# Raw output-weight loads issued from GpSimd's queue, and a seventh key buffer, in a one-core Trainium2 decoder layer

## The chip, the cores and the metric

The kernel runs on one core of one Trainium2 chip. The metric is device time in microseconds (us). A core has five engines with an instruction stream each: TensorE (PE in the profile; PEld are its weight loads), VectorE (DVE), ScalarE (ACT), GpSimd (POOL) and SyncE (SP). Each stream is worked off in order. An instruction may carry a wait for another engine or for a load, and everything behind it in the same stream waits too. In this kernel SP does nothing but issue loads and stores.

## The reference

One layer of a decoder trunk, on x of 2048 rows and 1024 columns, in float32. Cut to what matters here:

```python
h = rmsnorm(x, pre_norm_g)
q, k, v, g_attn, x_lru, g_lru = split(h @ w_in)          # 1024 columns each
y_attn = rmsnorm(diff_attention(q, k, v, lam)) * silu(g_attn)   # 8 heads, causal, two score maps a head
y_lru  = rg_lru(conv4(x_lru), gates) * silu(g_lru)        # 8 blocks of 128 channels
y = concat([y_attn, y_lru]) @ w_out                       # (2048, 2048) x (2048, 1024)
out = x + rmsnorm(y, post_norm_g)
```

## The kernel before

Every matmul operand is split into a high and a low part, and three products are added. Work is divided into 128-row tiles and 512-column chunks.

The kernel's stages, in order of time in the profile: normalisation and projections of the first half of the rows (0 to 600 us), the first half's attention with the second half's projections filled in between (to about 1144), the second half's recurrent part (`lru_run`, to 1382), the second half's attention with the output projection filled in between (1387 to about 2140), and the rest of the output projection (to the end).

Three things matter for the change.

*Output weights.* `load_wo(r, nh, k)` loads a tile of 128 rows and 512 columns into `woraw` (two buffers, line 950), and POOL splits it into `woh` (line 70) and `wol` (line 71). Eight of them (k = 0 to 7, one buffer each) are a set. There are four sets, in the order of `wsets`: (1, 0), (1, 1), (0, 0), (0, 1). The first is loaded beside the recurrent part (the program's scheduler moves it up to about 1144 us, the end of the first attention). Each other set is loaded during the last group of matmuls of the set before it, tile by tile as the old tile falls free, and the next group (line 1048, 24 matmuls in `fill_out`) reads it. The 49 groups run as fill between the attention's own instructions.

*Keys.* `load_k(h, j)` loads the keys of head h, positions 512 j to 512 j + 511, into one of `kbufs` buffers of the tag `ks`; a head has four such tiles in a ring. Scores (line 642) read them; the first score unit of a head in the second half reads tiles 0, 1 and half of tile 2 (that last matmul has 256 columns).

*Other work of POOL.* It splits the weights of the input projection (`wlo`, line 200, while DVE makes `whi`), the output projection's inputs (`yh`, `yl`, lines 70 and 71, in four parts a tile), and scales the attention's output (`yt`, line 782).

The order within each engine is fixed when the program is built: a scheduler places the instructions by its own model of their times and the buffers' availability. On the chip each engine keeps to that order.

Of the kernel before, what the change touches and what calls it, by code (L numbers as in the profile page):

```python
# [18 lines left out]
P = 128  # L19
S = 2048  # L20
D = 1024
KC = D // P
H = 8
CH = 512
# [10 lines left out]
FB = 8.25  # L35
# [8 lines left out]
def hymba_kernel(  # L44
# [6 lines left out]
    nc = tc.nc  # L51
    x2, out2, w_in2, w_out2 = x[0], out[0], w_in[0], w_out[0]
# [16 lines left out]
    def split(hi, lo, src):  # L69
        nc.gpsimd.tensor_scalar(out=hi, in0=src, scalar1=1.0, scalar2=1.0, op0=ALU.mult, op1=ALU.mult)  # L70
        nc.gpsimd.tensor_tensor(out=lo, in0=src, in1=hi.bitcast(F32), op=ALU.subtract)  # L71
# [875 lines left out]

    def load_wo(r, nh, k):
        raw = f_p.tile([P, CH], F32, tag="woraw", name="woraw", bufs=2)
        nc.sync.dma_start(out=raw, in_=w_out2[r * D + k * P:r * D + (k + 1) * P, nh * CH:(nh + 1) * CH])  # L950
        hi = f_p.tile([P, CH], F32R, tag=f"woh{k}", name=f"woh{k}", bufs=1)
        lo = f_p.tile([P, CH], F32R, tag=f"wol{k}", name=f"wol{k}", bufs=1)
        split(hi, lo, raw)
        wo[r, nh, k] = (hi, lo)

    def load_y(r, i):
        raw = f_p.tile([P, 8, P], F32, tag="yraw", name="yraw", bufs=YR)
        nc.sync.dma_start(out=raw, in_=(ya_s, yl_s)[r][i // 4][:, :, (i % 4) * P:(i % 4 + 1) * P])
        yh = f_p.tile([P, 8, P], F32R, tag="yh", name="yh")
        yl = f_p.tile([P, 8, P], F32R, tag="yl", name="yl")  # L960
        return (yh, yl), [(yh[:, k:k + 2], yl[:, k:k + 2], raw[:, k:k + 2]) for k in range(0, 8, 2)]
# [3 lines left out]
    def finish(pool, i, yv, bufs, halves, eng):  # L965

        ss = pool.tile([P, 6], F32, tag="ss", name="ss", bufs=6)

        def squares(c):
            s = slice(c * CH, (c + 1) * CH)  # L970
            junk = pool.tile([P, CH], F32, tag="fo", name="junk", bufs=bufs)
            nc.scalar.activation(out=junk, in_=yv[:, s], func=AF.Square, accum_out=ss[:, (5, 0)[c]:(6, 1)[c]])
            eng.tensor_tensor(out=yv[:, s], in0=yv[:, s], in1=pgt[:, s], op=ALU.mult)

        def rest():
            xt = pool.tile([P, D], F32, tag="xt", name="xt", bufs=bufs)
            nc.sync.dma_start(out=xt, in_=x2[i * P:(i + 1) * P, :])
            squares(0)
            nc.vector.tensor_tensor(out=ss[:, 0:1], in0=ss[:, 0:1], in1=ss[:, 5:6], op=ALU.add)
            rsqrt1(ss, D)  # L980
            for c0 in range(0, D, D // halves):
                s = slice(c0, c0 + D // halves)
                nc.vector.scalar_tensor_tensor(  # L983
                    out=xt[:, s], in0=yv[:, s], scalar=ss[:, 3:4], in1=xt[:, s], op0=ALU.mult, op1=ALU.add,
                )
                nc.sync.dma_start(out=out2[i * P:(i + 1) * P, s], in_=xt[:, s])

        squares(1)
        return rest

    with tc.tile_pool(name="lruB", bufs=2) as lp, tc.tile_pool(name="ps_pB", bufs=4, space=PSUM) as ps_p, \
            tc.tile_pool(name="ps_gB", bufs=1, space=PSUM) as ps_g:
        load_gw, lru_run = lru_tools(lp, ps_p, ps_g, 1)
        load_gw(0)
        pos = len(lightB)
        end = None
        for n in range(NB):
            wB.split(pos)
            wB.split(pos + 1)
            end = lru_run(n, wB, pos, end)  # L1000
            if n >= 4:
                load_wo(1, 0, 2 * (n - 4))
                load_wo(1, 0, 2 * (n - 4) + 1)
            pos += 2
        p1.close()
        end()
# [4 lines left out]
    with ExitStack() as pb:  # L1011
        kvB_p = pb.enter_context(tc.tile_pool(name="kvB", bufs=2, side="right"))
        e_p = pb.enter_context(tc.tile_pool(name="expB", bufs=2, side="right"))
        a_p = pb.enter_context(tc.tile_pool(name="attB", bufs=2, side="right"))
        ps_s = pb.enter_context(tc.tile_pool(name="ps_sB", bufs=4 * CH // SP, space=PSUM))
        ps_w = pb.enter_context(tc.tile_pool(name="ps_wB", bufs=2, space=PSUM))
        ps_o = pb.enter_context(tc.tile_pool(name="ps_oB", bufs=1, space=PSUM))
        ps_f = pb.enter_context(tc.tile_pool(name="ps_fB", bufs=1, space=PSUM))
        groups = [(r, nh, i) for r, nh in wsets for i in range((8, 16)[r])] + [(0, 1, 8)]

        def fill_out():
            ysp, parts = load_y(*groups[0][::2])
            for p in parts:
                split(*p)
            nc.sync.dma_start(out=pgt, in_=post_norm_g[0].partition_broadcast(P))
            for g, (r, nh, i) in enumerate(groups):
                ps = ps_f.tile([P, CH], F32, tag="f", name="f")
                yh, yl = ysp
                nxt = groups[g + 1] if g + 1 < len(groups) else None
                if nxt:  # L1030
                    ysp, parts = load_y(*nxt[::2])
                part = None
                c0 = nh * CH
                if i >= 8 and r == 0:
                    yv = f_p.tile([P, D], F32, tag="yv", name="yv", bufs=1)
                    nc.sync.dma_start(out=yv, in_=part_s[1][i])
                    part = yv[:, CH:]
                    ys[i], yvs[i] = ysp, yv
                elif r == 0:
                    if nh:  # L1040
                        yv = f_p.tile([P, D], F32, tag="yv", name="yv", bufs=1)
                        nc.sync.dma_start(out=yv[:, 0:CH], in_=part_s[0][i][:, 0:CH])
                    part = f_p.tile([P, CH], F32, tag="part", name="part", bufs=1)
                    nc.sync.dma_start(out=part, in_=part_s[1][i][:, c0:c0 + CH])
                for k in range(8):
                    hi, lo = wo[r, nh, k]
                    for m, (a, b) in enumerate(((yh, hi), (yl, hi), (yh, lo))):
                        nc.tensor.matmul(  # L1048
                            out=ps, lhsT=a[:, k, :], rhs=b, start=(k == 0 and m == 0), stop=(k == 7 and m == 2),
                        )  # L1050
                        if (k, m) != (7, 2):
                            yield
                    if nxt and nxt[:2] != (r, nh):
                        load_wo(*nxt[:2], k)
                    if k % 2 and nxt:
                        split(*parts[k // 2])
                if r == 0 and nh == 1:
                    nc.vector.tensor_tensor(out=yv[:, CH:], in0=ps, in1=part, op=ALU.add)  # L1058
                    ends[i] = finish(f_p, i, yv, 1, 1, nc.gpsimd if i < FE else nc.vector)
                    if i < 8:  # L1060
                        ends.pop(i)()
                else:
                    st = f_p.tile([P, CH], F32, tag="fo", name="fo", bufs=1)
                    if part:
                        nc.vector.tensor_tensor(out=st, in0=ps, in1=part, op=ALU.add)
                        nc.sync.dma_start(out=part_s[0][i][:, 0:CH], in_=st)
                    else:
                        nc.scalar.activation(out=st, in_=ps, func=AF.Copy)
                        nc.sync.dma_start(out=part_s[1][i][:, c0:c0 + CH], in_=st)
                yield "group"  # L1070

        attention(
            range(4, 8), kvB_p, e_p, a_p, ps_s, ps_w, ps_o, 4 * CH // SP, fill_out(),
            lambda s: FB if s > 1 else 6, 6, 5, 1,
        )


# [2 lines left out]
    with ExitStack() as p3:  # L1080
# [39 lines left out]
        for i in range(9, 12):  # L1120
            for k in ((0, 1, 2), (3, 4, 5), (6, 7))[i - 9]:
                raw = y_p.tile([P, CH], F32, tag="woraw3", name="woraw3")
# [45 lines left out]
```

## Time and profile before

| | |
|---|---|
| median of 3 runs | 2308.39 us (2305.96 to 2310.14) |
| the profiled execution | 2304.31 us, span 2302.5 us |
| PE busy | 2182.0 us, 95% |
| DVE busy | 1481.0 us, 64% |
| ACT busy | 984.2 us, 43% |
| POOL busy | 805.6 us, 35% |
| mean granted clock of PE | 0.981 of full |

The span is the profiled execution's; its own time is 1.8 us longer. Busy shares are means over stages. PE is the engine that is nearly always busy, so the rows below are about the stretches in which it is not, or in which its clock is at the lower of its two levels (1.2 instead of 2.4 GHz; 0.50 in the rows means that level throughout).

### The profile page before, as it was taken

Reading aid. Unit: us, or ns where it says so; the run is one execution under the profiler, and the core shown is the slowest. Engines: PE = TensorE matmul, PEld = TensorE weight load, DVE = VectorE, ACT = ScalarE, POOL = GpSimd, SP = SyncE. Lnnn points to the kernel's source line nnn. Section 1 sums busy time; section 2 is a strip of 40 time slices with the busy share of each in tenths; the row PEclk is TensorE's granted clock in tenths of the full one; section 3 lists DMA queues with packets and bytes.
Section 4 is the critical chain, followed back from the end, with each engine's and each line's share of the span. In section 5 each row is a group of like instructions: output and inputs, shape, how many; then the busy total and the mean of one; then the engine's idle time right before and its main releaser. Section 6 shows DMA issues by size and latency. Waiting matters only on the chain. (4 is left out here: it accounts for less than half of the span.)

```text
span 2302.5 us, 31830 instructions
## 1 busy us (share of the span) xinstructions
PE 2182.0 (95%) x11281; PEld 1800.5 (78%) x11281; DVE 1481.0 (64%) x2976; ACT 984.2 (43%) x2227; POOL 805.6 (35%) x773
## 2 busy tenths in 40 slices
PE   7999999999899999999999997999999997999778
PEld 6888888888677878888878775888788886887666
DVE  6531145446576666666337776888878886888565
ACT  4311134435443444444126564665565654555211
POOL 1222034445311111111275553133534335245452
PEclk9999999999999999999999998999999998999889
DMA  6554322332568777874462117457466475655473
GB/s 206 152 149 151 111 84 85 105 107 67 151 155 172 169 178 175 183 165 115 121 183 69 62 34 178 105 145 166 117 156 165 111 147 133 170 138 146 110 260 128
DMA packets 358783, 317.93 MB, mean 138 GB/s; under 512 B 32545, under 2 KB 290658, under 8 KB 358626
## 3 DMA queue, kind: packets, MB, share of 16 engines
q1 hardware_dynamic: 358626, 315.91, 52.8%
q8 instruction: 89, 1.46, 0.3%
q14 instruction: 68, 0.56, 0.1%
HBM read 221.41 MB, written 94.44 MB: 137 GB/s over the span
## 5 line engine op out<-in xcount | busy, mean ns | idle before, releaser
L228 PE MATMUL ps<-hh,whi 128*128 128x512 f32 (+1 forms) x1456 | 569.3, 391 | 3.7 <-DVE hilo L245 3.0
L228 PE MATMUL ps<-hh,wlo 128*128 128x512 f32 (+1 forms) x1456 | 567.1, 390 | 0.0
L228 PE MATMUL ps<-hl,whi 128*128 128x512 f32 (+1 forms) x1456 | 565.0, 388 | 1.1 <-DVE hl L446 1.1
L683 ACT ACTIVATE p<-s,nm 128x512 f32<-128x512 f32 (+3 forms) x640 | 392.0, 623 | 330.4 <-DVE nm L667 221.3
L665 DVE TENSOR_REDUCE mx<-s 128x1 f32<-128x512 f32 (+3 forms) x576 | 341.4, 618 | 115.4 <-PE s L642 95.3
L642 PE MATMUL s<-ks,qs 128*128 128x512 f32 (+2 forms) x1280 | 368.8, 386 | 33.7 <-DMA ks<-k_s 18.7
L200 POOL TENSOR_TENSOR wlo<-wraw,whi 128x1024 fp32r<-128x1024 f32 x88 | 222.5, 2529 | 438.6 <-DVE whi L199 136.3
L228 PEld LDWEIGHTS ps<-hh,whi 128*128 128x128 f32 x1456 | 277.3, 190 | 55.0 <-DVE hilo L245 3.8
L228 PEld LDWEIGHTS ps<-hl,whi 128*128 128x128 f32 x1456 | 276.9, 190 | 52.5 <-DVE hl L446 1.4
L228 PEld LDWEIGHTS ps<-hh,wlo 128*128 128x128 f32 x1456 | 276.6, 190 | 51.2
L642 PEld LDWEIGHTS s<-ks,qs 128*128 128x128 f32 x1280 | 215.7, 191 | 86.8 <-ACT p L683 36.3
L719 ACT ACTIVATE wh<-pw 128x512 fp32r<-128x512 f32 (+1 forms) x288 | 160.1, 577 | 184.9 <-PE pw L715 181.5
L738 PE MATMUL o<-wh,vs 128*128 128x256 f32 (+1 forms) x1152 | 223.5, 284 | 0.8 <-ACT wh L719 0.8
L720 DVE TENSOR_TENSOR wl<-pw,wh 128x512 fp32r<-128x512 f32 (+1 forms) x288 | 185.7, 654 | 35.9 <-ACT wh L719 34.6
L738 PEld LDWEIGHTS o<-wh,vs 128*128 128x128 f32 x1152 | 193.6, 192 | 19.1 <-ACT wh L719 3.3
L70 POOL TENSOR_SCALAR yh<-yraw 128x256 fp32r<-128x256 f32 x196 | 89.9, 476 | 288.8 <-PE f L1048 265.8
L1048 PE MATMUL f<-woh,yh 128*128 128x512 f32 x392 | 163.3, 417 | 22.1 <-DVE yv L1058 16.1
L782 POOL TENSOR_TENSOR yt<-yt,rb 128x512 f32<-128x512 f32 x32 | 41.8, 1307 | 406.0 <-DMA rb<-r_s 224.0
L701 DVE SCALAR_TENSOR_TENSOR p<-p,rr,p 128x128 f32<-128x128 f32 (+15 forms) x128 | 180.2, 1407 | 2.8
L715 PE MATMUL pw<-ident,p 128*128 128x128 f32 x1088 | 169.2, 274 | 4.1 <-DVE wl L720 2.6
L738 PE MATMUL o<-wl,vs 128*128 128x256 f32 x576 | 164.4, 286 | 9.1 <-DVE wl L720 9.1
L1048 PE MATMUL f<-wol,yh 128*128 128x512 f32 x392 | 163.3, 416 | 0.9 <-POOL wol L71 0.9
(166 smaller groups left out, 3316.9 us busy)
## 6 DMA issues: line engine op xcount, KB each, us to landing
wraw<-in_w_in_dram SPq DMA_DIRECT2D x96, 512.0 KB, 5.0
qs<-q_s SPq DMA_DIRECT2D x128, 256.0 KB, 5.5
vs<-v_s SPq DMA_DIRECT2D x48, 512.0 KB, 6.2
ks<-k_s SPq DMA_DIRECT2D x96, 256.0 KB, 5.6
xt<-in_x_dram SPq DMA_DIRECT2D x32, 512.0 KB, 4.7
k_s<-hilo SPq DMA_DIRECT2D x64, 256.0 KB, 4.1
q_s<-hilo SPq DMA_DIRECT2D x64, 256.0 KB, 3.8
v_s<-hilo SPq DMA_DIRECT2D x32, 512.0 KB, 3.7
```

Source lines behind the costliest of these rows:

```text
L70: nc.gpsimd.tensor_scalar(out=hi, in0=src, scalar1=1.0, scalar2=1.0, op0=ALU.mult, op1=ALU.mult)
L200: nc.gpsimd.tensor_tensor(out=lo, in0=src, in1=hi.bitcast(F32), op=ALU.subtract)
L228: nc.tensor.matmul(out=ps[:, t0:t0 + n], lhsT=a[:, k, :], rhs=b[:, k, t0:t0 + n], start=(k == 0 and m == 0), stop=(k == KC - 1 and m == 2),)
L642: nc.tensor.matmul(out=ps[:, b0 - c0:b0 - c0 + nk], lhsT=qq[:, c, t * P:(t + 1) * P], rhs=kst[h, b0 // CH][:, c, 0:nk], start=(m == 0), st ...
L665: nc.vector.tensor_reduce(out=mx[:, pi:pi + 1], in_=sc[u, pi][:, 0:c1 - c0], axis=AX.X, op=ALU.max)
L683: nc.scalar.activation(out=p[:, c0:c1], in_=sc.pop((u, pi))[:, 0:c1 - c0], func=AF.Exp, bias=negm[u], accum_out=acc,)
L701: nc.vector.scalar_tensor_tensor(out=p0[:, 0:n], in0=p1[:, 0:n], scalar=rr[:, 1:2], in1=p0[:, 0:n], op0=ALU.mult, op1=ALU.add,)
L715: nc.tensor.transpose(pw[:, i * P:(i + 1) * P], wts[h, pr, t][:, kb * P:(kb + 1) * P], ident)
L719: nc.scalar.activation(out=wh[:, 0:n], in_=pw[:, 0:n], func=AF.Copy)
L720: nc.vector.tensor_tensor(out=wl[:, 0:n], in0=pw[:, 0:n], in1=wh[:, 0:n].bitcast(F32), op=ALU.subtract,)
L738: nc.tensor.matmul(out=po[h, j][:, oo:oo + w1 - w0], lhsT=a[:, kb % 4, :], rhs=w[:, w0:w1], start=(kb == 0 and m == 0), stop=(kb == 2 * pr ...
L1048: nc.tensor.matmul(out=ps, lhsT=a[:, k, :], rhs=b, start=(k == 0 and m == 0), stop=(k == 7 and m == 2),)
```

## The change

Two edits. The raw load of an output weight tile is issued by GpSimd, not by SyncE. And the second half's attention gets seven buffers for key tiles instead of six (`kbufs`, the argument behind the lambda).

```diff
     def load_wo(r, nh, k):
         raw = f_p.tile([P, CH], F32, tag="woraw", name="woraw", bufs=2)
-        nc.sync.dma_start(out=raw, in_=w_out2[r * D + k * P:r * D + (k + 1) * P, nh * CH:(nh + 1) * CH])
+        nc.gpsimd.dma_start(out=raw, in_=w_out2[r * D + k * P:r * D + (k + 1) * P, nh * CH:(nh + 1) * CH])
...
         attention(
             range(4, 8), kvB_p, e_p, a_p, ps_s, ps_w, ps_o, 4 * CH // SP, fill_out(),
-            lambda s: FB if s > 1 else 6, 6, 5, 1,
+            lambda s: FB if s > 1 else 6, 7, 5, 1,
         )
```

How the program's order moves, at three places. PE's order and ACT's stay as they were.

SP, where the third set of output weights is loaded (in time, about 1915 us), in the program before; `ks` with k_s_2_118 is key tile 2 of the head that starts there:

```order
L950 DMA woraw<-in_w_out_dram 128x512
L958 DMA yraw<-ya_s_196 128x8x128
L950 DMA woraw<-in_w_out_dram 128x512 x6
L1069 DMA part_s_15_227<-fo 128x512
L950 DMA woraw<-in_w_out_dram 128x512
L623 DMA gt<-g_s_2_158 128x512
L600 DMA ks<-k_s_2_118 64x1024 x2
```

SP of the change, where that same key tile's load stands now:

```order
L785 DMA ya_s_198<-yt 128x512
L600 DMA ks<-k_s_1_117 64x1024
L600 DMA ks<-k_s_2_118 64x1024 x2
L1069 DMA part_s_11_223<-fo 128x512
L616 DMA qs<-q_s_3_83 64x4x256 x2
L958 DMA yraw<-yl_s_203 128x8x128
```

The key tile's load has moved ahead by four groups of the output projection (part_s_11 against part_s_15 are the stores of groups 11 and 15), and the weight loads have left SP.

POOL, at the first set's end (about 1163 to 1180 us), before; the two `wlo` are those of the second and third column block of the recurrent part:

```order
L71 TENSOR_TENSOR wol_12061<-woraw,woh_12060 128x512
L200 TENSOR_TENSOR wlo<-wraw,whi 128x1024
L70 TENSOR_SCALAR woh_12066<-woraw 128x512
L71 TENSOR_TENSOR wol_12067<-woraw,woh_12066 128x512
L70 TENSOR_SCALAR yh<-yraw 128x256 x2
L71 TENSOR_TENSOR yl<-yraw,yh 128x256 x2
L70 TENSOR_SCALAR yh<-yraw 128x256 x2
L71 TENSOR_TENSOR yl<-yraw,yh 128x256 x2
L200 TENSOR_TENSOR wlo<-wraw,whi 128x1024
```

POOL of the change, the same place:

```order
L950 DMA woraw<-in_w_out_dram 128x512 x2
L71 TENSOR_TENSOR yl<-yraw,yh 128x256
L70 TENSOR_SCALAR yh<-yraw 128x256
L71 TENSOR_TENSOR yl<-yraw,yh 128x256
L70 TENSOR_SCALAR woh_12060<-woraw 128x512
L71 TENSOR_TENSOR wol_12061<-woraw,woh_12060 128x512
L70 TENSOR_SCALAR woh_12066<-woraw 128x512
L950 DMA woraw<-in_w_out_dram 128x512
L71 TENSOR_TENSOR wol_12067<-woraw,woh_12066 128x512
L950 DMA woraw<-in_w_out_dram 128x512
L200 TENSOR_TENSOR wlo<-wraw,whi 128x1024 x2
```

The second block's `wlo` now stands behind all eight splits and ten loads (the last two already belong to the second set). All y splits stand before it too.

POOL, where the fourth set is loaded (about 2057 us), before:

```order
L70 TENSOR_SCALAR woh_20028<-woraw 128x512
L71 TENSOR_TENSOR wol_20029<-woraw,woh_20028 128x512
L70 TENSOR_SCALAR woh_20037<-woraw 128x512
L71 TENSOR_TENSOR wol_20038<-woraw,woh_20037 128x512
L70 TENSOR_SCALAR woh_20075<-woraw 128x512
L71 TENSOR_TENSOR wol_20076<-woraw,woh_20075 128x512
L70 TENSOR_SCALAR woh_20112<-woraw 128x512
```

POOL of the change, the same place:

```order
L70 TENSOR_SCALAR woh_20028<-woraw 128x512
L71 TENSOR_TENSOR wol_20029<-woraw,woh_20028 128x512
L70 TENSOR_SCALAR woh_20037<-woraw 128x512
L950 DMA woraw<-in_w_out_dram 128x512
L71 TENSOR_TENSOR wol_20038<-woraw,woh_20037 128x512
L950 DMA woraw<-in_w_out_dram 128x512
L70 TENSOR_SCALAR woh_20075<-woraw 128x512
L71 TENSOR_TENSOR wol_20076<-woraw,woh_20075 128x512
L950 DMA woraw<-in_w_out_dram 128x512
L70 TENSOR_SCALAR woh_20112<-woraw 128x512
```

One load is issued for each tile split, in between the splits; the first two tiles of the set have been loaded long before. At the third set the pattern is the same.

## Rows read from the trace of the kernel before

**Rows 1.** The page: span, and busy time of each engine.

```profile
span 2302.5 us, 31830 instructions
...
PE 2182.0 (95%) x11281; PEld 1800.5 (78%) x11281; DVE 1481.0 (64%) x2976; ACT 984.2 (43%) x2227; POOL 805.6 (35%) x773
```

**Rows 2.** PE's waits, 1480 to 2130 us: total, times, longest.

```profile
PE s L642 <- DMA ks<-k_s: 15.4, 4, 11.0
...
PE f L1048 <- POOL wol L71: 0.9, 1, 0.9
```

**Rows 3.** Timeline of PE: two waits for keys (start, us, instruction, [idle before]).

```profile
1660.01 0.47 PE L642 MATMUL s<-ks,qs 128*128 128x256 f32 x2 [1.65 <-DMA ks<-k_s]
...
1942.57 0.77 PE L642 MATMUL s<-ks,qs 128*128 128x256 f32 x2 [11.02 <-DMA ks<-k_s]
```

**Rows 4.** Timeline of SP's issues, third set.

```profile
1917.39 14.91 SPq L950 DMA_DIRECT2D woraw<-in_w_out_dram  x6
...
1936.16 1.11 SPq L600 DMA_DIRECT2D ks<-k_s  x2
```

**Rows 5.** Stretches: length, busy PE, PEld, DVE, ACT, POOL, PEclk, DMA share, GB/s.

```profile
1932.00:1943.00 11.00, 0.43 (x2) 0.46 (x2) 1.67 (x6) 0.00 (x0) 6.09 (x10) 0.57 0.79 204
1943.00:1948.00 5.00, 5.00 (x22) 4.49 (x22) 4.45 (x10) 1.79 (x6) 0.00 (x0) 0.58 1.24 164
```

**Rows 6.** The tile woraw: durations in ns (min/median/max), then landing.

```profile
L950 SPq DMA_DIRECT2D woraw<-in_w_out_dram x32: 327/333/1472, 1144.0 to 2072.9; - x32
L70 POOL TENSOR_SCALAR woh<-woraw x32: 610/618/1471, 1147.9 to 2077.8; 128x512 fp32r<-128x512 f32 x32
L71 POOL TENSOR_TENSOR wol<-woraw,woh x32: 1261/1289/3071, 1149.3 to 2078.8; 128x512 fp32r<-128x512 f32 x32
...
DMA to landing us min/median/max: 2.5/3.4/6.6
```

**Rows 7.** Timeline of SP's issues, first set.

```profile
1143.98 0.82 SPq L950 DMA_DIRECT2D woraw<-in_w_out_dram  x2
```

**Rows 8.** Timeline of POOL, first set.

```profile
1154.02 0.77 POOL L70 TENSOR_SCALAR yh<-yraw 128x256 fp32r<-128x256 f32 x2
1154.76 1.40 POOL L71 TENSOR_TENSOR yl<-yraw,yh 128x256 fp32r<-128x256 f32 x2
...
1170.40 2.40 POOL L200 TENSOR_TENSOR wlo<-wraw,whi 128x1024 fp32r<-128x1024 f32 x1
```

**Rows 9.** Timeline of PE, first set and the recurrent part's start.

```profile
1156.33 0.79 PE L228 MATMUL ps<-hh,whi 128*128 128x512 f32 x1 [3.05 <-DVE hilo L245]
...
1181.38 0.39 PE L228 MATMUL ps<-hh,wlo 128*128 128x512 f32 x1
...
1193.40 0.47 PE L315 MATMUL pg<-xch,gwh 128*128 128x512 f32 x1 [1.44 <-ACT xc L297]
1194.71 0.51 PE L315 MATMUL pg<-xcl,gwh 128*128 128x512 f32 x1 [0.83 <-POOL xcl L200]
```

**Rows 10.** Timeline of POOL: ends and starts of the reload chains.

```profile
1664.39 1.28 POOL L71 TENSOR_TENSOR wol<-woraw,woh 128x512 fp32r<-128x512 f32 x1
...
1913.41 0.62 POOL L70 TENSOR_SCALAR woh<-woraw 128x512 fp32r<-128x512 f32 x1
...
1934.01 1.26 POOL L71 TENSOR_TENSOR wol<-woraw,woh 128x512 fp32r<-128x512 f32 x1
...
2057.21 0.63 POOL L70 TENSOR_SCALAR woh<-woraw 128x512 fp32r<-128x512 f32 x1
...
2078.76 1.29 POOL L71 TENSOR_TENSOR wol<-woraw,woh 128x512 fp32r<-128x512 f32 x1
```

**Rows 11.** Timeline of PE: the last matmul that takes each reloaded set.

```profile
1672.48 0.39 PE L1048 MATMUL f<-wol,yh 128*128 128x512 f32 x1
...
1949.48 0.39 PE L1048 MATMUL f<-wol,yh 128*128 128x512 f32 x1
...
2080.11 0.50 PE L1048 MATMUL f<-wol,yh 128*128 128x512 f32 x1 [0.87 <-POOL wol L71]
```

**Rows 12.** Stretches behind the waits of 3.05 and 1.65 us; columns as in rows 5.

```profile
1155.00:1162.00 7.00, 5.67 (x13) 4.46 (x14) 1.38 (x2) 1.14 (x2) 6.83 (x7) 0.52 0.64 219
...
1660.00:1670.00 10.00, 9.60 (x53) 7.61 (x53) 9.01 (x19) 3.76 (x12) 8.83 (x10) 1.00 0.80 155
```

## The prediction

> **What bounds the kernel now.** I read the page first. TensorE (PE) is busy 95% of a 2302.5 us span [rows 1]. PE takes its instructions in order, so what can still be won or lost is where PE stands still, and how much slower it runs afterwards. The change touches two things: loads on SP's queue and work on GpSimd (POOL). So I next asked who PE waits for in the second half's attention (1480 to 2130 us). Keys lead by far: 15.4 us in 4 waits, the longest 11.0; the other row of that table that matters below is wol, 0.9 us [rows 2]. Two of the four key waits are shown: 1.65 us at 1658 and 11.02 us before 1942.57 [rows 3]. Both rows are a score matmul of 256 columns, which is key tile 2 at a head's start.
>
> Why is that tile late? There are four key tiles a head in one ring. With six slots tile 2 of head h takes the slot of tile 0 of head h-1, which is read until that head's last score unit: the load can't go out before the head ends. At 1932 something is added: SP sits on six raw output weight loads for 14.91 us, and the keys behind them go out at 1936.16 [rows 4]. Six issues are six times 0.333 us [rows 6], 2.0 of the 14.91; the rest is SP waiting until POOL has split the tile that holds the raw buffer. So the queue was held by a wait, not by issuing. After the gap PE ran at the lower clock level: the granted clock is 0.57 and 0.58 in the two stretches from 1932 to 1948 [rows 5].
>
> **What goes away.** With seven slots tile 2 of head h takes the slot of tile 3 of head h-2, free for a whole head. SP's order in the new program bears this out: that load stands in the middle of the previous head, far ahead of the weight reload. I take all four waits as gone: **-15.4 us**. The clock comes back too: from 1942.57 to about 1947.2 PE worked 4.6 us at the half level, which at full level is 2.3 us: **-2.3 us**. What is late next there is the weight reload itself, costed below. Together -17.7.
>
> **What is added: 32 issues on POOL.** Each raw load is now an instruction in POOL's own stream, and that stream is also the consumer (woh, wol). The trace of before has no load issued by POOL, so I bound its time there. Below: 0.33 us, the issue of the same load on SP [rows 6]. Above: 2.40 us, POOL's longest pass (wlo, 1024 columns) [rows 8]. In between lie POOL's passes over this very tile, 0.62 us with one input and 1.29 with two [rows 6]. A list has to be written for 128 lines on both sides, and these two are the nearest rows, so I take their middle, rounded to **1.0 us** (an estimate). From issue to landing SP's loads need 3.4 us at the median [rows 6], 3.07 after the issue; I keep 3.07 behind the 1.0.
>
> Now the four places where a set of eight tiles is loaded. Per tile POOL works 0.66 + 1.30 = 1.96 us. Set two, around 1650, hides the change: its last wol ends at 1665.67 [rows 10] and PE takes it at 1672.48 [rows 11], 6.8 us later. The other three don't hide it.
>
> **First set, 1144 to 1187.** The raw loads were first issued at 1143.98 [rows 7]; on POOL they can't be earlier, as the memory comes free then. In the new order POOL does, from there to the end of the second recurrent projection's wlo, 10 issues, 8 splits, two 4-part y tiles (2 x (0.77 + 1.41) = 4.3 us each) and 3 wlo at 2.40 [rows 8]: 10 x 1.06 (0.06 for the hand-over) + 15.7 + 8.7 + 7.2 = 42.2, and about 0.3 of waiting for landings. It ends at 1186.5; before it ended at 1172.8 [rows 8]. PE wants it at 1181.38 [rows 9]: 5.1 us late. Behind it PE had two waits of its own, 1.44 and 0.83 us for the convolution [rows 9], which doesn't hang on that wlo and gets ready meanwhile. Net **+2.8 us**. The clock: the nearest wait, 3.05 us at 1153 [rows 9], was followed by 7 us at a clock of 0.52 with PE busy 5.67 [rows 12], half of which, **+2.8 us**, I charge here.
>
> **Third set, 1913 to 1936.** The chain took from 1913.41 to 1935.27 [rows 10]. I go through POOL's new order step by step: a buffer is free after a wol, then 1.06 for the issue, 3.07 to land, then 0.66 and 1.30; two buffers. The eight wol end at 1915.4, 1918.4, 1922.5, 1926.3, 1929.3, 1932.3, 1935.4 and 1939.5 (in front of the last stand an issue of the next set and two y parts). PE's last matmul of that group started at 1949.48 [rows 11]; take off the 11.02 wait and 2.3 of clock and PE wants the tile at 1936.2: **+3.3 us**, in pieces of 0.3 to 1.5.
>
> **Fourth set, 2057 to 2080.** The chain took from 2057.21 to 2080.05 [rows 10], and PE already caught up with it: its last matmul of the group waited 0.87 us for the last wol [rows 11]. There is no slack. By the same steps the wol end at 2059.2, 2062.2, 2065.9, 2068.9, 2072.0, 2075.0, 2078.1 and 2083.3 (five y parts in front of the last): **+3.2 us**. I charge no clock for sets three and four: their pieces are no longer than the wait of 1.65 us in [rows 3], and behind that one the clock was 1.00 [rows 12].
>
> **Sum.** -15.4 - 2.3 + 2.8 + 2.8 + 3.3 + 3.2 = -5.6 us. On the profiled execution, 2304.3 us (its span and 1.8 around it), that is 2298.7. The median of the three runs shown, 2308.39, lies 4.1 higher, so for the runs I forecast **2302.8**. The same sum for other prices of an issue, all else kept: 0.33 us gives -16 (the first set hides it, third and fourth lose 0.3 and 1.2); 0.62 gives -14; 1.29 gives 5.5 + 2.8 + 5.0 + 4.6 = 17.9 of loss, +0.2; 2.40 gives 16.6 + 2.8 + 12.3 + 10.8 = 42.5, +25.
>
> **Two rules that speak against the change.** The Trainium skill, DMA: Bandwidth & Descriptors, "Issuing engines are not separate DMA queues", says that loads from any engine run on the same 16 DMA engines, and that issuing from another only saves the issuing sequencer's time, which is usually small. By that rule the move gives 32 x 0.333 = 10.7 us of SP's time and nothing of PE's, so that only its costs on POOL remain. By it the sum would be that of the third rival, +6.2 instead of -5.6. The row with 14.91 us disagrees: what SP spends there is waiting in front of the keys, and that goes with the move. The Trainium skill, SBUF — State Buffer, "Who interferes with whom", says that GpSimd can be kept from generating a load's descriptors while VectorE runs in its two-port modes. No row here shows it; it would make the issue dear (the second rival).
>
> **The rivals.**
> *A cheap issue.* At 0.33 to 0.7 us POOL's idle time takes most of it. For it: SP does the same in 0.33 us [rows 6]; against it: POOL's cheapest pass over this tile takes 0.62. Time: 2308.4 - 14 = 2294. Chance 25%.
> *A dear issue: slower.* POOL becomes the bound in the three reloads. From about 1.3 us the losses reach 17.7 and the gain is gone. At 1.6 us: 8.6 + 2.8 + 6.8 + 6.1 = 24.3, and some 1.5 for the clock: +8.1, 2316.5. For it: POOL's two-input passes took up to 3.07 us where the median is 1.29 [rows 6], so anything on POOL can stretch; VectorE is busy there. Against it: an issue reads no tile. Chance 20%. (By the skill's second rule the time would land here.)
> *The move frees nothing.* SP is held by another wait (it also waits for POOL's y splits, which now come later) and the keys stay behind it. If only the three short key waits go, the 9.5 us that the long one has above their mean of 1.5 and the clock's 2.3 stay: +6.2, 2314.6; if none goes, +12.1, 2320.5. Against it: the load's new place is some 25 rows of SP ahead of the reload. Chance 5%. (The skill's first rule lands here, at +6.2.)
>
> **How the numbers follow.** The forecast's own case (0.7 to 1.3 us) has 50% and runs from -13 to 0, 2295 to 2308.5. The range takes the cheap case in full, to -17, and the dear one to +8.5: 2291 to 2317; beyond it lie the dearest issues and the lost keys. A difference of 0.2%, 4.6 us, is about what a measurement of this kernel can tell from no change. Faster than that: the cheap case and a bit over half of my own, 52%. Within it: the rest of my own and the start of the dear case, 26%. Slower: 22%.
>
> **What would show it.** In the profile after: no PE wait for ks in 1480 to 2130 (right for the keys); woraw as POOL's DMA issues, with their duration (the price); PE waits for wlo near 1181, and for woh and wol in the third and fourth reload, some 3 to 5 us each; a lower clock behind the first. I am wrong if the issue is far from 1.0 us, if a load lands much later than 3 us behind it, or if the place of the ks wait is taken by another one at the head's start.

## The result and the profile after

The changed kernel takes 2322.0 us (median of 6 runs, 2315.6 to 2326.7) against 2307.4 for the kernel before, measured beside it (6 runs, 2301.4 to 2310.1): a ratio of 1.0063, 95% interval 1.0048 to 1.0077. It is slower by 0.6%, above the forecast range and on the other side of the forecast.

The page of the kernel after, to be read beside [rows 1]: the span, PE's and POOL's work, and a DMA queue that the page of before doesn't have.

```profile
span 2321.9 us, 31835 instructions
...
PE 2194.3 (95%) x11281; PEld 1808.4 (78%) x11281; DVE 1482.2 (64%) x2976; ACT 984.5 (42%) x2227; POOL 824.9 (36%) x805
...
q0 software_dynamic: 2560, 8.39, 1.2%
```

POOL has 32 instructions and 19.3 us more. PE executes the same 11281 matmuls in the same order, so the two traces can be laid on each other matmul by matmul. Now PE's waits in 1480 to 2130 us, against [rows 2].

```profile
PE f L1048 <- POOL woh L70: 6.3, 5, 2.0
PE f L1048 <- DVE fo L1065: 5.9, 1, 5.9
PE s L642 <- ACT p L683: 3.9, 3, 3.3
PE f L1048 <- ACT fo L1068: 3.6, 4, 2.1
PE pw L715 <- DVE wl L720: 2.5, 2, 1.8
PE f L1048 <- POOL wol L71: 2.4, 4, 1.2
```

The row for ks (15.4 us) is gone. In its place stand woh and wol, which were 0.9 us in one row, and fo: the next group of matmuls has to wait until the sums of the last one (f) have been read out, by ACT (line 1068) or, from the third set on, by DVE (line 1065), which adds a tile `part` that SP loads. The tile woraw, against [rows 6]:

```profile
L950 POOL DMA_DIRECT2D woraw<-in_w_out_dram x32: 536/584/851, 1143.9 to 2088.9; - x32
...
  POOL woraw L950: 5.6, 19
...
DMA to landing us min/median/max: 2.5/4.4/8.9
```

An issue takes POOL 0.58 us, and before 19 of them POOL waited for its own last wol, 0.30 us each. By this row the loads land 1.0 us later at the median than in [rows 6], at worst 2.3 later. The two rows compare unequal samples: the trace of before places the landing of only 12 of these 32 loads, and both rows also hold loads of the last stage, which SP issues in either kernel. What that does to a reload is seen in POOL's timeline, second set (start, us, instruction, [idle before]):

```profile
1667.61 0.58 POOL L950 DMA_DIRECT2D woraw<-in_w_out_dram  x1 [0.30 <-POOL wol L71]
1668.63 0.61 POOL L70 TENSOR_SCALAR woh<-woraw 128x512 fp32r<-128x512 f32 x1 [0.44 <-DMA woraw<-in_w_out_dram]
1669.32 1.29 POOL L71 TENSOR_TENSOR wol<-woraw,woh 128x512 fp32r<-128x512 f32 x1
1670.91 0.59 POOL L950 DMA_DIRECT2D woraw<-in_w_out_dram  x1 [0.30 <-POOL wol L71]
1676.68 0.61 POOL L70 TENSOR_SCALAR woh<-woraw 128x512 fp32r<-128x512 f32 x1 [5.19 <-DMA woraw<-in_w_out_dram]
```

The load of 1667.61 is split at 1676.68, nine us later. This is the set that was to hide the change: its last wol ends at 1682.45, 16.8 us later than before [rows 10], and PE takes it 0.06 us later. In this set POOL waits 7.5 us for raw loads. From the first woh to the last wol the four sets now take 34.5, 32.3, 29.1 and 28.8 us; before 26.9, 22.7, 21.9 and 22.8.

And SP? Its waits in the kernel after, 1936 to 1961 us, and its issues there, against [rows 4]:

```profile
SPq L958 <- POOL yh L70: 20.7, 1, 20.7
```

```profile
1937.58 1.19 SPq L616 DMA_DIRECT2D qs<-q_s  x2
1959.18 0.53 SPq L958 DMA_DIRECT2D yraw<-ya_s  x1
1959.76 0.67 SPq L600 DMA_DIRECT2D ks<-k_s  x1
1960.52 0.54 SPq L773 DMA_DIRECT2D r_s<-f  x1
...
1972.34 0.84 SPq L1044 DMA_DIRECT2D part<-part_s  x1
```

SP was held 14.9 us in front of woraw; now it is held 20.7 us in front of yraw, which waits for POOL's y splits, and these are later because POOL is slower. No key is late in this, but the part load is, which stands behind it and behind a further wait of 7.7 us for the store r_s: that is the wait of 5.9 us for fo.

### The profile page after: what moved, and what is told of

It is laid out like the page before. It is cut to its first block, busy times and chain, and to the rows that moved or that the text cites. A ratio compares the mean times of both kernels' runs of the same rounds, so it can differ in the third digit from the quotient of the medians.

```text
span 2321.9 us, 31835 instructions
## 1 busy us (share of the span) xinstructions
PE 2194.3 (95%) x11281; PEld 1808.4 (78%) x11281; DVE 1482.2 (64%) x2976; ACT 984.5 (42%) x2227; POOL 824.9 (36%) x805
## 5 line engine op out<-in xcount | busy, mean ns | idle before, releaser
L70 POOL TENSOR_SCALAR yh<-yraw 128x256 fp32r<-128x256 f32 x196 | 95.8, 505 | 264.7 <-PE f L1048 208.4
```

## The experiments

All times are medians; the kernel before was measured beside each experiment and stood at 2308.8 to 2310.8 us. A ratio, with its 95% interval, is worked out over all runs and can differ a little from that of the medians.

**e1_keys7: the seventh key buffer alone.**

```diff
-            lambda s: FB if s > 1 else 6, 6, 5, 1,
+            lambda s: FB if s > 1 else 6, 7, 5, 1,
```

> Seven key buffers alone, the raw loads left on SyncE's queue. Theory A (the stall at a head's start is a missing buffer: with six buffers a new head's third key can only be asked for when the old head ends, with seven it is asked for a head earlier, so what SyncE's queue holds up then does not matter): all four waits for ks of rows 2 go, also the one of 11.02 us, so 2307 - 15 - about 2 of clock = 2289 to 2293 us. Theory B (the prediction's: the wait of 11.02 us comes from SyncE's queue being held by woraw for 14.9 us): only the short waits go, 4.4 us, and the long one stays: 2301 to 2305 us. Theory C (the seventh buffer itself costs, by loads that collide with others): 2307 us or more.

Measured: 2295.7 us against 2310.8, ratio 0.9946 (0.9926 to 0.9967). Its PE waits in 1480 to 2130 us begin like this:

```profile
PE pw L715 <- DVE wl L720: 4.8, 3, 2.6
PE f L1048 <- DVE fo L1065: 3.5, 1, 3.5
PE s L642 <- ACT p L683: 2.5, 3, 1.6
```

No key wait is left, the long one included, though SP still sits on woraw there. Theory A holds, with a little less gain than it named; for the keys, what SP's queue holds up doesn't matter once the third one is asked for a head earlier. This kernel is the fastest of the study: the gain is all the buffer's.

**e2_pool6: the move alone.** The changed kernel with 6 key buffers.

> The raw loads on GpSimd's queue, six key buffers as before. Theory A (the queue move costs, the buffer pays): the move costs about 35 us (measured +14.7, with the 15 us for keys taken out again), less what the freed SyncE queue takes off the long key wait (11.0 down to about 1.5): 2328 to 2342 us, waits for ks of a few us in all. Theory B (the freed queue is what removes the long key wait, and the move costs 30): 2326 us, with only 4 us of waits for ks. Theory C (the buffer costs): 2315 us or less.

Measured: 2323.5 us, ratio 1.0067 (1.0045 to 1.0090). PE's waits of this kernel, same stretch:

```profile
PE f L1048 <- POOL woh L70: 11.1, 6, 4.7
PE f L1048 <- POOL wol L71: 3.5, 5, 1.2
...
PE s L642 <- DMA ks<-k_s: 2.8, 2, 1.5
```

The move too takes the long key wait away (1.5 us is left of 11.0). So both edits remove the same stall, and together they can remove it only once: with the loads on POOL, six buffers (1.0067) and seven (1.0063) can't be told apart. The time lies under both A's and B's, so this run alone doesn't part them; with e1 it is plain that the buffer needs no move.

**e3_first_sp and e4_half_sp: the move taken back set by set**, at seven buffers. In e3 the first set's loads are back on SP, in e4 the first and the second set's.

```diff
-        nc.gpsimd.dma_start(out=raw, ...
+        (nc.sync if (r, nh) == (1, 0) else nc.gpsimd).dma_start(out=raw, ...    # e3
+        (nc.sync if r else nc.gpsimd).dma_start(out=raw, ...                    # e4
```

> The changed kernel with only the first weight set's eight raw loads back on SyncE's queue. Theory A (the first set's slower chain on GpSimd holds up yraw and, behind it on SyncE, the stores that free hilo near 1170, and the same delay is what lengthens the start of the second attention near 1410): both steps go, 5.8 and 3.7 us, so 2322 - 9.5 = 2312 us (2309 to 2315). Theory B (the step near 1410 has another cause, the freed SyncE queue): only 5.8 goes, 2316 us. Theory C (the first set costs nothing in the end because later waits absorb it): 2320 to 2324 us.

> The changed kernel with the first and second weight sets' sixteen raw loads back on SyncE's queue, the third and fourth on GpSimd's. Theory A (each set on GpSimd costs by its slower reload chain): the second set's 8.4 us goes too: 2322 - 9.5 - 8.4 = 2304 us (2300 to 2308). Theory B (the second set's step comes from the shift of the program ahead of it, not from its own chain): 2311 to 2314 us.

Measured: e3 2317.3 us, ratio 1.0034 (1.0017 to 1.0051); e4 2308.2 us, ratio 0.9995 (0.9981 to 1.0009). With e1 and the changed kernel this is a ladder: e1 2295.7, third and fourth set on POOL +12.5, the second too +9.1, the first too +4.8, the changed kernel 2322.0. These are differences of medians, each good to some 3 to 5 us, and the last one sets a kernel beside another that was measured at another time: against the kernel before, measured beside each, it would be 8.2. The first set's step fits e3's theory B better than A: the longer start of the second attention near 1405 us (PE waits 5.7 us there in e1 and 5.8 in e4, 1.4 in the kernel before) is there without the move, so the move doesn't make it, and neither does a freed SP queue, which B names and e1 doesn't have. The step from e3 to e4 is that of theory A, though e4 itself ends 0.2 us above its range. In e3 the second set's load of 1663.61 again lands nine us later and the set takes 31.3 us, in e4 21.1. PE's order is the same in all of these, so their profiled executions can be laid on each other, each pair differing in one place: the first set then costs 2.5 us (e3 to the changed kernel, 1150 to 1500 us), the second 6.0 (e4 to e3), the third and fourth 5.6 and 6.1 (e1 to e4).

**e5_pool6_raw4 and e6_sp6_raw4: four raw buffers**, on POOL's queue and on SP's, with six key buffers. The raw tiles get pools of their own, which delays the first set by some 37 us in both (its first woh at 1183 and 1186 us), so the two are compared with each other first.

```diff
-        raw = f_p.tile([P, CH], F32, tag="woraw", name="woraw", bufs=2)
+        raw = raws[-1].tile([P, CH], F32, tag="woraw", name="woraw", bufs=2 if r and not nh else 4)
```

> The raw loads on GpSimd's queue with six key buffers, and four raw buffers in place of two for the second to the fourth weight set. Each raw load is then issued two tiles earlier, so neither its landing nor GpSimd's wait for its own last subtraction (0.30 us) stands in the reload chain. Theory A (the chain is slow because landing and own wait stand in it): a tile takes about 1.95 of splitting and 0.58 of issue, a set about 20 us instead of 29 to 32, less than the 22.7 on SyncE's queue, and the waits for woh and wol (14.6 us) go: 2323 - 10 to - 18 = 2305 to 2313 us. Theory B (issuing on GpSimd itself is the price): sets stay near 27 to 30 us and the time at 2318 to 2324 us.

> The kernel before (raw loads on SyncE's queue, six key buffers) with four raw buffers for the second to the fourth set. Theory A: the chain of a set falls from 22.7 to some 16 to 18 us, SyncE's queue is held for woraw about 8 us less near 1920, so the key wait of 11.0 us falls to 2 to 5: 2307 to 2311 - 6 to - 10 = 2298 to 2304 us. Theory B (the wait is bound to the old head's end, whatever the queue does): 11 us stay, 2306 to 2311 us.

Measured: e5 2314.6 us, ratio 1.0027 (1.0012 to 1.0043); e6 2307.8 us, ratio 0.9991 (0.9977 to 1.0005). In e5 the sets two to four take 21.6, 21.7 and 19.1 us instead of 34.1, 31.9 and 27.9 in e2, PE's rows for woh and wol are gone, and 8.8 us come back in spite of the later first set: theory A as to the chain, the time a little above its range. Laid on e2, PE wins 3.8 us at the second set, 1.9 at the third and 3.7 at the fourth. In e6 the sets take 17.2 to 17.9 us and the long key wait falls from 11.0 to 7.5: the queue has a part in it, but a smaller one than theory A says, and the time is in theory B's range. With the landing out of the chain the move still costs 6.9 us (e5 against e6).

**e7_pool6_y3: a third yraw buffer**, on e2 (every third yraw tile from a pool of its own, which also changes PE's order in a stretch of some 450 matmuls from 1422 us on).

> The raw loads on GpSimd's queue with six key buffers, and a third buffer for yraw. Theory A (with the raw loads gone, SyncE's queue is held by yraw waiting for GpSimd's splits, 20.7 us at the third set, and what stands behind it is late): the long yraw wait shortens by the time of one block, the time falls from 2323 to 2312 to 2319 us. Theory B (PE's own waits for woh and wol carry the loss, yraw's does not): 2321 to 2326 us.

Measured: 2318.6 us, ratio 1.0042 (1.0028 to 1.0057); the interval overlaps that of e2. The longest wait of SP for yh is 22.5 us, as in e2 (22.2). The time lies in theory A's range, but the mechanism that A named didn't happen, so the run doesn't support it, and whether the 4.9 us are real stays open.

**e8_dummy: 24 small loads issued by POOL, nothing else moved**, at seven buffers.

```diff
+        dm = f_p.tile([P, 16], F32, tag="dm", name="dm", bufs=4)
+        if (r, nh) != (1, 0):
+            nc.gpsimd.dma_start(out=dm, in_=w_out2[r * D + k * P:r * D + (k + 1) * P, nh * CH:nh * CH + 16])
```

> Seven key buffers with the raw loads on SyncE's queue, and beside each of the 24 loads of the second to fourth set GpSimd issues one load of 128 x 16 values that nobody reads. It prices the issue on GpSimd without the raw loads' wait and landing. Theory A (the wait and the landing in the chain make most of the loss of about 26 us): 24 issues of 0.55 us lengthen three chains by 4.4 us, of which half reaches PE: 2296 + 2 to 7 = 2298 to 2303 us. Theory B (the issue itself is the price): 2296 + 12 to 20 = 2308 to 2316 us.

Measured: 2310.0 us, ratio 1.0008 (0.9994 to 1.0022), 14.3 above e1. But these loads wait for no split, and the scheduler put all 24 far ahead of their sets, as their tile's row shows (first and last start):

```profile
L953 POOL DMA_DIRECT2D dm<-in_w_out_dram x24: 534/536/737, 1146.2 to 1183.6; - x24
```

So the time lies in theory B's range, but the run answers another question: what 24 issues cost in the stage of the first set. Laid on e1, PE loses 13 us there between 1150 and 1200 us and little afterwards: POOL's time in that stage reaches the kernel. The price of one issue doesn't follow, since 24 issues of 0.54 us make 12.9 and POOL also waited 7.0 there for buffers of the small loads and for memory. That 14.3 / 24 x 8 is 4.8, the first set's step on the ladder, is no more than consistent.

**e10_dummy_late: the same price at the right places.** Each small load now reads the wol just written, so that it stands behind it in POOL's order.

```diff
+        if (r, nh) != (1, 0):
+            dm = f_p.tile([P, 16], F32R, tag="dm", name="dm", bufs=8)
+            nc.gpsimd.dma_start(out=dm, in_=lo[:, 0:16])
```

> Seven key buffers with the raw loads on SyncE's queue, and behind each of the 24 subtractions of the second to fourth set GpSimd issues one small load from its result (128 x 16 values, read by nobody), at the places where the changed kernel's raw loads stand. It is the issue (about 0.55 us) with the wait for GpSimd's own subtraction (0.30 us), without the raw loads' landing behind it. Theory A (the landing standing in the chain carries the loss of sets two to four, 21.6 us): chains grow from 21 to 23 us to some 24 to 26, and the time by 2 to 7: 2298 to 2303 us. Theory B (GpSimd's own 0.9 us a tile carries it): chains of 27 to 29 us, 2296 + 14 to 20 = 2310 to 2316 us.

Measured: 2310.3 us, ratio 1.0004 (0.9993 to 1.0015), 14.7 above e1. The tile dm and POOL's timeline in the second set:

```profile
L956 POOL DMA_DIRECT2D dm<-wol x24: 568/598/752, 1645.2 to 2084.2; - x24
...
  POOL wol L71: 4.8, 16
```

```profile
1653.79 1.27 POOL L71 TENSOR_TENSOR wol<-woraw,woh 128x512 fp32r<-128x512 f32 x1
1655.36 0.60 POOL L956 DMA_DIRECT2D dm<-wol  x1 [0.30 <-POOL wol L71]
1655.99 0.63 POOL L70 TENSOR_SCALAR woh<-woraw 128x512 fp32r<-128x512 f32 x1
1656.71 1.29 POOL L71 TENSOR_TENSOR wol<-woraw,woh 128x512 fp32r<-128x512 f32 x1
```

From one wol to the next pass 2.92 us a tile instead of the 1.96 of splitting alone. The sets take 23.3, 26.2 and 27.3 us, the theory between A and B; the time is B's. Laid on e1, matmul by matmul, PE loses 1 us at the second set and 6 each at the third and fourth. So POOL's own time is enough for a loss of the size of the third and fourth set's steps, and not for the second's. It reaches PE by partly other waits: in e10 for fo at the third set (8.1 us; 3.5 in e1) and for yv, another addition of DVE's that needs a load, at the fourth (5.3); in e4 for woh and wol (4.3 and 4.2) beside fo (5.1). That the changed kernel's two steps are this price alone is therefore argued, not shown. For the second set the difference is what e10 leaves out, the landing: POOL waits 7.5 us for raw loads in that set in the changed kernel, 1.7 in e1 and never in e10. e5, which takes the landing out of the chain, wins there too.

**e9_act7: ScalarE's queue instead of POOL's**, at seven buffers.

```diff
-        nc.gpsimd.dma_start(out=raw, ...
+        nc.scalar.dma_start(out=raw, ...
```

> Seven key buffers, the raw loads issued from ScalarE's queue. GpSimd then issues nothing, SyncE's queue is free of woraw, but ScalarE's own work (exponentials, evictions) stands behind each raw load that waits for GpSimd's subtraction, 43.7 us of such waits in 1640 to 2110 on SyncE's queue in the kernel with seven buffers. Theory A (a queue in whose order waiting loads stand pays on what is behind them; on ScalarE that is the softmax that TensorE waits for): 2296 + 8 to 30 = 2304 to 2326 us, with waits of PE for p of L683 and fo of L1068 above the 7.4 and 2.1 us of seven buffers alone. Theory B (only GpSimd's own time matters, any other queue is free): 2292 to 2299 us.

Measured: 2323.0 us, ratio 1.0054 (1.0041 to 1.0066). ACT's waits in 1100 to 2110 us name what is held up:

```profile
ACT wh L719 <- POOL wol L71: 21.0, 4, 7.4
...
ACT p L683 <- POOL wol L71: 11.4, 3, 7.0
```

ACT sits in front of a raw load until POOL has split, and softmax work stands behind it: in 1390 to 2200 us PE waits 20.7 us for p (7.4 in e1) and 7.8 for fo (2.1). Theory A. An issue took 0.33 us there; it is the waiting that costs.

## Why the prediction was wrong

**What held.** The keys: all four waits went, by the mechanism given (the seventh slot), -15.2 us in e1 where -17.7 was forecast. Part of it is given back at once: with the 11 us gone PE meets the part load and waits 3.5 us for fo near 1962. The first set: +4.8 against +5.6, which is luck, as it came by another road. No wait for the wlo near 1181 appeared, PE being late already; in front of it PE waited for hilo, and from inside that wait on, 1171.8 to 1178.5 us, its granted clock was 0.50:

```profile
1174.23 0.79 PE L228 MATMUL ps<-hh,whi 128*128 128x512 f32 x1 [4.55 <-DVE hilo L247]
```

SP had waited for POOL's yl in front of a yraw load, and behind it stood the k_s stores that free hilo (SP's waits, 1150 to 1176 us):

```profile
SPq L958 <- POOL yl L71: 11.4, 1, 11.4
```

The price of an issue, 1.0 plus 0.06: measured 0.58 plus 0.30 of waiting for POOL's own wol, in e10 2.92 - 1.96 = 0.96 a tile. Right in sum and wrong in its parts, so luck again; taken at the bare 0.58, the price table would have forecast a larger gain. (The upper bound, 2.40 us, was not POOL's longest pass: [rows 6] has one of 3.07.)

**The step that failed first: "Set two, around 1650, hides the change".** It set 6.8 us of slack against no figure: eight tiles at 1.06 more make 8.5, and the step-by-step working of sets three and four was left out for this one. Yet by e10 the issues alone would nearly have been hidden: with issue and self-wait in its chain the set takes 23.3 us, 2.4 more than in e1, and PE loses 1. The term that failed is the landing. 3.07 us behind the issue was assumed; it was 8.3 (8.9 from the issue's start) for the load that decided, and the set took 32.3. With two buffers, a late landing holds the whole loop. Forecast 0; measured 9.1 by the medians of e3 and e4, 6.0 by their traces.

**The second: the losses of sets three and four, for which "I charge no clock".** Forecast +6.5, measured +12.5 (e4 against e1). The chains grew more than worked out (26.1 us each in the forecast; 29.1 and 28.8 measured, landing included). The pieces did cost clock: behind the wait of 1.97 us for woh at 1945.77 the granted clock fell to the half level for 6.8 us. The rule drawn from one wait of 1.65 us without such a fall was too much to hang on one row. Here are the stretches around the three reloads, first of the kernel after, then of e1 (length, busy PE, PEld, DVE, ACT, POOL, PEclk, DMA share, GB/s):

```profile
1655.00:1700.00 45.00, 41.56 (x237) 34.25 (x236) 32.70 (x71) 22.94 (x63) 26.80 (x37) 0.92 0.52 128
1915.00:2000.00 85.00, 75.81 (x435) 63.18 (x434) 60.45 (x122) 42.09 (x113) 47.87 (x66) 0.92 0.69 164
2050.00:2120.00 70.00, 66.14 (x383) 54.99 (x383) 60.70 (x122) 36.07 (x100) 42.66 (x55) 0.98 0.52 132
```

```profile
1655.00:1700.00 45.00, 42.01 (x258) 35.26 (x258) 37.61 (x72) 24.84 (x68) 26.38 (x33) 1.00 0.77 201
1915.00:2000.00 85.00, 78.02 (x459) 65.16 (x458) 68.52 (x141) 44.51 (x122) 37.44 (x51) 0.98 0.64 165
2050.00:2120.00 70.00, 66.80 (x380) 55.02 (x379) 64.34 (x136) 40.85 (x113) 44.78 (x55) 0.98 0.59 158
```

In the first two PE is busy almost as long and starts 45 matmuls fewer (672 against 717): 0.92 against 1.00 and 0.98. The windows are equal in time, not in work, as the kernel after is 7 to 25 us behind e1 in them. How the 6.0 us that are missing divide between chains, clock and the wait for fo wasn't separated.

**The sum again.** -15.2 (keys) + 4.8 + 9.1 + 12.5 = +11.2, where -17.7 + 5.6 + 0 + 6.5 = -5.6 was forecast. The four terms are differences of neighbouring medians, so that they add up is no test of them; against the kernel before as measured beside it, the changed kernel is at +14.7. The tests are other: e10 makes a loss of 6 us each at the third and fourth set, and almost none at the second, by another edit, and the traces place 2.5, 6.0, 5.6 and 6.1 us at the four sets.

**The rivals.** The cheap issue came true as a price and not as a time. The dear one didn't come: no issue took over 0.85 us, and the Trainium skill's rule on VectorE's two-port modes (SBUF — State Buffer, "Who interferes with whom") shows in no stretched issue here; whether it has a part in the later landings wasn't separated. Of the third rival, "the move frees nothing", one half is right: SP is held by POOL's y splits instead, and longer. The other half is not, since the keys were no longer behind it. And the rule named with it: the Trainium skill, DMA: Bandwidth & Descriptors, "Issuing engines are not separate DMA queues", has loads from any engine on the same DMA engines and only the issuing sequencer's time to be won. With seven buffers it has held: that time was in nobody's way (e1), and the loads landed no earlier (4.4 us against 3.4). With six, the move also took the long key wait away (e2, 11.0 to 1.5), a wait in the queue and not issuing time. In the prediction the row of 14.9 us was held against that rule; it showed what held the keys at six buffers, not what would hold them at seven.

**What stays open.** Why the second set's loads landed late. The one of 1667.61 was issued 0.25 us behind the normaliser's store r_s (2 KB, issued at 1667.36), which landed 9.0 us after its issue, while in 1668 to 1677 us the DMA moved only 50 GB/s. The other traces show the same: over the six kernels with raw loads on GpSimd, the 12 that were issued within 7 us behind an r_s store landed after 8.2 to 13.2 us, the other 156 after 4.2 at the median (four of them after more than 8). So it is with SP's key loads in the kernels before and after and in e1, as far as the traces place their landing: 20 were issued that way and landed after 8.3 to 14.3 us, the others after 5.3 to 5.5 at the median. This fits a store that holds up what is issued behind it from either queue; but it is a coincidence in time, and no kernel without the store at that place was run. Nor do the traces place the whole of e1's gain: the profiled execution of e1 (2299.4 us) lies above the median of its runs and that of before (2304.3) below its own, 4.9 apart instead of 15.2. Laid on each other they differ by 12.4 us at the long key wait, of which 7.3 are lost again by 1970 us.

## What to carry to other kernels

When two edits aim at one stall, run each alone: here either removed the long key wait, one at no cost that shows in the time, the other for 26 to 30 us. Moving a load that waits for a consumer's buffer onto the consumer's own queue puts its issue and its self-wait into the chain, and the landing stays there: add them up for every place where the chain is reloaded, the comfortable ones too, and with a late landing (8.9 us here, 4.4 at the median), before calling one hidden. A queue that waits is freed by asking earlier (a buffer), and moved to another engine it holds up that engine's work instead.

## What the runs showed of the hardware

GpSimd's issue of a 256 KB load took 0.54 to 0.85 us in the changed kernel (0.95 at most in e2), of a 128 x 16 one 0.53 to 0.75 (e8, e10); both have 128 lines, and their length hardly mattered. A GpSimd instruction that issues a load waited 0.30 us for GpSimd's own previous instruction, where a pass over the same tile followed within 0.1 us (1668.63 + 0.61, then 1669.32). SyncE issued the same load in 0.33 us, ScalarE too.
